# A decoder layer in split fp32: the order of the twelve matmuls in a product

## The chip, the cores and the metric

The kernel runs on one core of a Trainium2 chip. A core has a matrix engine (TensorE, PE in the profile, with its weight loads in a row of their own, PEld), a vector engine (VectorE, DVE), a scalar engine (ScalarE, ACT), a general engine (GpSimd, POOL) and a queue engine (SyncE, SP) that issues most transfers. The engines run side by side, each through its own instructions in order, and wait for one another on semaphores. The metric is the device time of one execution in microseconds, the median of several runs.

## The reference

One layer of a decoder over 2048 positions of width 1024, in fp32. Modulated input, a wide projection, two mixers side by side (sliding-window attention and a causal pool), gates, an output projection and a layer norm:

```python
u = x * (1.0 + scale[:, None, :]) + shift[:, None, :]
h = u @ w_in[l]
q, k, v, a_gate, p_in, p_gate, m_a, m_p = jnp.split(h, offsets, axis=-1)
a = sliding_window_sink_attention(q, k, v, sinks[l], bias, mask) * jax.nn.silu(a_gate)
a = a @ w_attn_proj[l]
p = jnp.einsum('bsgc,gcd->bsgd', multiscale_causal_pool(p_in), w_pool_mix[l]).reshape(B, S, POOL_WIDTH)
p = (p * pool_scale[l]) * jax.nn.silu(p_gate)
p = p @ w_pool_proj[l]
y = jax.nn.sigmoid(m_a) * a + jax.nn.sigmoid(m_p) * p
y = (y @ w_out[l]) * (1.0 + gate[:, None, :])
x = layer_norm(DEEPNORM_ALPHA * x + y, ln_gain[l], ln_bias[l])
```

Nearly all the time goes to the dense products: `u @ w_in` (seven groups of 1024 columns' worth of output tiles and a small k/v group), the two projections and the output product.

## The kernel before

**Split numbers.** TensorE works on fp32r operands here. An fp32 operand is split in two: a high part, rounded by a copy to fp32r (on ACT), and a low part, the rest (`low`, line 130, a subtraction on DVE or POOL). A product of two split operands takes three matmuls: high by high, high by low, low by high (`mm3`, line 136).

**Seven products instead of eight.** A `Quad` (line 244) holds two 128-row weight tiles over the contraction of 1024, and multiplies them with 1024 positions. Seen as blocks it is two by two by two; it is done in the Strassen-Winograd manner with seven block products, named after the moving side's blocks: B11, T1, T2, B21, T3, B22, T4. For each name there is a `set_...` tile in SBUF with four k-tiles, each with a high and a low part of 512 columns. The weight side is summed by POOL (`sum1`, `mid`, `late`) into tile `W` and then split: `pair_split` (line 303) casts 128x1024 numbers on ACT (line 305) and takes the low part on DVE (line 131 by way of 306), into two `w_set` tiles that serve two products each; `half_split` (line 309) does so for one product. There are four `w_set` buffers, used in turn, so a cast waits until PE has read an old tile for the last time.

**A product.** `product` (line 316) multiplies one block: four k-tiles, three matmuls each, twelve matmuls of 128x128 weights by 128x512, all into one PSUM bank (`mm` or `lg` in the profile). Before the change it goes k-tile by k-tile and calls `mm3` for each, so that the weight's low part is first read by the third matmul.

**Stages.** The positions are done in two halves. For each half a ring of gate projections (`first_phase`, `second_phase`) is followed by attention, into whose PE stream the products of 13 further quads are filled, one k-tile at a time (`filling`, which calls `product` with `k, k + 1`). The last stage, from about 1190 us on, has the two projections of each half and the output product. In rings `front` opens a quad (B11, T1), `back` goes on with T2, B21, T3, B22, T4 for two quads in turn, and `finish_pairs` ends the output product. Lines 367, 389 and 420 are DVE adds that read finished products, and each quad's `consume` reads its results out of PSUM.

**What sets the order.** Work beside the products (loads, set splits, sums, stores) hangs on ticks, one per product. PE's instructions keep the order in which the program writes them: all go through `pe`, an `Ordered` wrapper (line 50) that pins each behind the one before. So do calls through `act`, `dve`, `pool` and `sp`. Calls written as `nc.scalar`, `nc.vector`, `nc.gpsimd` and `nc.sync`, which is what `pair_split`, `half_split`, `front`, `back` and most consumers use, are not pinned: the framework's planner sorts them by its own estimate of when each is ready, in the program's order among the ready ones. Semaphore waits come from what each instruction reads and writes.

**Sets.** For each new phase, `set_steps` (line 493) fetches a set in two halves of two k-tiles, through SP, into the place of the old set's low parts, and splits it there. The fetch waits for PE's last read of the part it overwrites.

Of the kernel before, what the change touches and what calls it, by code (L numbers as in the profile page):

```python
# [19 lines left out]
P = 128  # L20
# [39 lines left out]
def kernel(  # L60
# [72 lines left out]
    def mm(*args, **kw):  # L133
        pe.matmul(*args, **kw)

    def mm3(acc, whi, wlo, uhi, ulo, start, stop, **kw):
        mm(acc, whi, uhi, start=start, stop=False, **kw)
        mm(acc, whi, ulo, start=False, stop=False, **kw)
        mm(acc, wlo, uhi, start=False, stop=stop, **kw)
# [176 lines left out]
    def product(acc, w, name, first=False, i0=0, i1=4):  # L316
        t = sets[name]
        hi, lo = w
        for i in range(i0, i1):
            cols = slice(i * P, (i + 1) * P)  # L320
            mm3(
                acc,
                hi[:, cols],
                lo[:, cols],
                t[:, i, 0, :],
                t[:, i, 1, :],
                first and i == 0,
                i == 3,
                skip_group_check=True,
            )  # L330

    def front(ph, q, tick):
        w = pair_split(ph, q.first())
        q.mid()
        a, b = bank(), bank()
        product(a, w[0], "B11", True)
        tick()
        product(b, w[1], "T1", True)
        tick()
        return a, b, None, None  # L340

    def back(ph, grp, opened, nxt, own, tick):
# [5 lines left out]
        for q, (a, b, c, w, *copy) in zip(grp, opened):  # L348
            p5 = ph.p("p5")
            if w is None:  # L350
                c = bank("lg")
                nc.scalar.copy(c, a)
                nc.scalar.copy(p5, b)
                w = pair_split(ph, q.second())[::-1]
                q.late()
                product(c, w[1], "T2")
            else:
                u2 = copy[0] if copy else ph.p("u2")
                if not copy:
                    nc.scalar.copy(u2, a)  # L360
                if c is None:
                    c = bank("lg")
                    product(c, w[1], "T2", True)
                nc.vector.tensor_tensor(c, c, u2, ALU.add)
                nc.scalar.copy(p5, b)
            tick()
            nc.vector.tensor_tensor(b, c, p5, ALU.add)
            if not copy:
                product(a, w[0], "B21")
            tick()  # L370
            q.consume(ph, 0, 0, a)
            st.append((q, b, c, p5))
# [1092 lines left out]
    with Pools("mix", spare=4, p=2, c=8) as ph:  # L1465
# [10 lines left out]
        for n, (raw, i) in enumerate((raw, i) for raw in (ain_d[1], pin_d[1], wo_d) for i in range(4)):  # L1476
            for offset, f in sums_to(ph, raw, i, load_raw(raw, i)):
                at = int(2 + 8 * n + offset)
                i, gi = every[at // 14]
# [78 lines left out]
```

## Time and profile before

| | |
|---|---|
| median of 3 runs | 1722.41 us (1721.44 to 1725.9) |
| the profiled execution | 1724.84 us, of which its span is 1723.1 |
| PE, matmuls | 8056, busy 1659.3 us (96%) |
| PEld, weight loads | 8056, busy 1389.4 us (81%) |
| DVE | busy 1283.1 us (74%) |
| ACT | busy 965.8 us (56%) |
| POOL | busy 1001.9 us (58%) |
| mean granted TensorE clock | 0.991 |

A row of a group names line, engine, operation, the tiles it writes and reads, shapes and count. In order of time a row gives the start, the length of a merged stretch, and in brackets the engine's idle time before it with what ended it. Most instructions are recorded at line 56, the wrapper's, so tiles tell them apart. Matmuls overlap: each is recorded with a length that is longer than the step from one start to the next.

### The profile page before, as it was taken

How to read it: one execution, taken by the hardware profiler on the slowest of the kernel's cores; microseconds unless marked ns; L12 is line 12 of the kernel's file. 1: busy time of each engine (PE TensorE's matmuls, PEld its weight loads, DVE VectorE, ACT ScalarE, POOL GpSimd, SP SyncE). 2: the span in 40 equal slices, each digit the busy share in tenths (PEclk: the TensorE clock that was granted, in tenths of full speed). 3: DMA queues.
4: the chain of work that ended last, by engine and by line, in shares of the span. 5: the costliest groups of instructions: out<-in, count | busy, mean ns of one | idle time of the engine just before them, and what ended most of it. 6: DMA issues, size and time to landing. Idle time of an engine off the chain costs nothing.

```text
span 1723.1 us, 24716 instructions
## 1 busy us (share of the span) xinstructions
PE 1659.3 (96%) x8056; PEld 1389.4 (81%) x8056; DVE 1283.1 (74%) x2288; ACT 965.8 (56%) x2002; POOL 1001.9 (58%) x750
## 2 busy tenths in 40 slices
PE   6899999999999999999999999999999989999996
PEld 5788888888888788887788888888777767778885
DVE  5966665787778768557578777786779886979877
ACT  4644446677677555334567776765645345434452
POOL 2054437686867837863376868595667575523442
PEclk9999999999999999999999999999999999999999
DMA  9388853333433468875533344234988896777442
GB/s 354 126 283 284 220 180 129 117 96 125 142 116 104 129 223 269 299 248 184 197 125 96 113 128 157 83 115 157 339 271 321 301 342 243 292 257 250 159 142 103
DMA packets 188850, 336.79 MB, mean 195 GB/s; under 512 B 18337, under 2 KB 44081, under 8 KB 188721
## 3 DMA queue, kind: packets, MB, share of 16 engines
q1 hardware_dynamic: 185600, 330.96, 56.5%
q10 hardware_dynamic: 3088, 4.23, 1.1%
q8 instruction: 64, 1.05, 0.3%
q14 instruction: 66, 0.53, 0.1%
q0 software_dynamic: 32, 0.02, 0.0%
HBM read 227.96 MB, written 110.33 MB: 196 GB/s over the span
## 4 chain that ended last, share of the span: by engine, by line
PE 44%; DVE 9%; DMA 6%; POOL 5%; issue 4%; ACT 1%; SPq 0%; POOLq 0%; DVEq 0%; ACTq 0%
PE mm L56 29%; PE lg L56 11%; DVE w_set L131 3%; PE pv L56 2%; PE pt L56 2%; DVE set_T L56 1%; POOL nxt L56 1%; POOL w_set L56 1%; DMA set_T<-ain_T 1%; DMA W<-y_d 1%; DVE set_B L56 1%; DVE wide L612 1%; POOL W L56 1%; POOL fin L56 1%; DMA g<-ma_d 1%
## 5 line engine op out<-in xcount | busy, mean ns | idle before, releaser
L56 PE MATMUL mm<-set_B,w_set 128*128 128x512 f32 x2664 | 658.5, 394 | 11.0 <-DVE w_set L131 10.6
L56 PEld LDWEIGHTS mm<-set_B,w_set 128*128 128x128 f32 x2664 | 498.2, 189 | 118.5 <-DVE w_set L131 15.2
L56 PE MATMUL mm<-set_T,w_set 128*128 128x512 f32 x1824 | 456.9, 396 | 4.4 <-POOL w_set L56 1.2
L56 PE MATMUL lg<-set_T,w_set 128*128 128x512 f32 x1728 | 420.5, 393 | 16.4 <-DVE w_set L131 9.0
L56 PEld LDWEIGHTS mm<-set_T,w_set 128*128 128x128 f32 x1824 | 336.8, 189 | 76.9 <-DVE mm L56 5.5
L56 PEld LDWEIGHTS lg<-set_T,w_set 128*128 128x128 f32 x1728 | 324.8, 189 | 90.8 <-DVE w_set L131 13.7
L131 DVE TENSOR_TENSOR w_set<-W,w_set 128x1024 fp32r<-128x1024 f32 x138 | 199.4, 1446 | 153.6 <-ACT w_set L305 143.1
L305 ACT CAST w_set<-W 128x1024 fp32r<-128x1024 f32 x138 | 144.9, 1050 | 258.6 <-PE mm L56 174.2
L56 POOL TENSOR_TENSOR w_set<-W,w_set 128x512 fp32r<-128x512 f32 x132 | 172.1, 1311 | 101.7 <-ACT w_set L56 94.5
L268 POOL TENSOR_TENSOR W<-W,A 128x512 f32<-128x512 f32 x46 | 71.0, 1543 | 252.4 <-ACT w_set L312 58.7
L56 ACT ACTIVATE L<-L,nm 128x257 f32<-128x257 f32 (+1 forms) x256 | 127.1, 498 | 25.8 <-DVE nm L56 20.0
L56 POOL TENSOR_TENSOR W<-W 128x512 f32<-128x512 f32 x82 | 108.4, 1336 | 51.6 <-DVE sm L56 30.3
L56 POOL TENSOR_TENSOR spare<-spare 128x512 f32<-128x512 f32 x68 | 122.4, 1803 | 23.8 <-DMA spare<-pin_B 10.3
L277 POOL TENSOR_TENSOR W<-W 128x512 f32<-128x512 f32 x46 | 69.2, 1504 | 108.8 <-DVE w_set L131 99.7
L56 DVE CUSTOM_DVE_ANT_0 L<-lg,bt,nsink 128x256 f32<-128x256 f32 (+1 forms) x256 | 111.7, 473 | 19.8 <-DMA bt<-e_rep 9.0
L56 ACT CAST w_set<-W 128x512 fp32r<-128x512 f32 (+1 forms) x164 | 100.1, 626 | 37.4 <-POOL W L56 25.8
L56 DVE COPY o<-pv 64x256 f32<-64x256 f32 x128 | 54.3, 424 | 82.3 <-PE pv L56 81.0
L272 POOL TENSOR_TENSOR W<-W 128x512 f32<-128x512 f32 x44 | 72.2, 1645 | 68.7 <-DVE w_set L131 59.7
L56 ACT CAST pth<-pt 128x512 fp32r<-128x512 f32 (+1 forms) x128 | 72.8, 569 | 63.0 <-PE pt L56 62.6
L56 ACT ACTIVATE L<-L,sm 128x256 f32<-128x256 f32 (+1 forms) x128 | 64.3, 503 | 67.9 <-DVE sm L56 67.7
L273 POOL TENSOR_TENSOR W<-W 128x512 f32<-128x512 f32 x44 | 79.3, 1803 | 30.7 <-DMA W<-in_win_dram 27.9
L56 DVE TENSOR_SCALAR L<-L,sm 128x256 f32<-128x256 f32 (+1 forms) x128 | 89.8, 702 | 0.0
(225 smaller groups left out, 2445.2 us busy)
## 6 DMA issues: line engine op xcount, KB each, us to landing
W<-in_win_dram SPq DMA_DIRECT2D x42, 512.0 KB, 5.6
W<-in_win_dram SPq DMA_DIRECT2D x42, 256.0 KB, 4.1
A<-in_win_dram SPq DMA_DIRECT2D x42, 256.0 KB, 4.8
ag_d<-sig SPq DMA_DIRECT2D x32, 256.0 KB, 5.2
pg_d<-sig SPq DMA_DIRECT2D x32, 256.0 KB, 4.8
pg<-pg_d SPq DMA_DIRECT2D x32, 256.0 KB, 3.2
pin_B<-fin SPq DMA_DIRECT2D x32, 256.0 KB, 2.1
ag<-ag_d SPq DMA_DIRECT2D x32, 256.0 KB, 3.0
```

Of the source, the lines that this page charges most:

```text
L56: return lambda *args, **kw: self.tc.keep_in_program_order(op(*args, **kw))
L131: engine.tensor_tensor(dst, src, as32(hi), ALU.subtract)
L268: e.tensor_tensor(self.w[:, 1, :], self.w[:, 2, :], self.a22, ALU.add)
L272: e.tensor_tensor(x[:, 1, :], x[:, 1, :], x[:, 0, :], ALU.subtract)
L273: e.tensor_tensor(x[:, 2, :], x[:, 0, :], x[:, 2, :], ALU.subtract)
L277: e.tensor_tensor(x[:, 3, :], x[:, 3, :], x[:, 1, :], ALU.subtract)
L305: a.copy(by_two(hi), raw)
L612: nc.vector.tensor_tensor(dst, g, dst, ALU.add)
```

## The change

`product` loops over the three kinds of matmul outside and over the k-tiles inside: first the high weight by the set's high part for all k-tiles, then the high weight by the set's low part, last the low weight by the set's high part. `start` and `stop` stay with the first and the last matmul. `mm3` is left to the small weight fold in the first stage.

```diff
     def product(acc, w, name, first=False, i0=0, i1=4):
         t = sets[name]
         hi, lo = w
-        for i in range(i0, i1):
-            cols = slice(i * P, (i + 1) * P)
-            mm3(
-                acc,
-                hi[:, cols],
-                lo[:, cols],
-                t[:, i, 0, :],
-                t[:, i, 1, :],
-                first and i == 0,
-                i == 3,
-                skip_group_check=True,
-            )
+        for n, (part, u) in enumerate(((hi, 0), (hi, 1), (lo, 0))):
+            for i in range(i0, i1):
+                mm(
+                    acc,
+                    part[:, i * P : (i + 1) * P],
+                    t[:, i, u, :],
+                    start=first and i == 0 and n == 0,
+                    stop=i == 3 and n == 2,
+                    skip_group_check=True,
+                )
```

A program run of the kernel calls `product` 324 times for a whole product of four k-tiles, 6 times for two or three of them (in the head), and 762 times for a single k-tile.

## The prediction

> **What bounds the kernel now.** I read the page first, then who waited for whom on PE, then PE's and DVE's instructions in order of time, then the chain of work that ended last.
>
> ```profile
> span 1723.1 us, 24716 instructions
> ...
> PE 1659.3 (96%) x8056; PEld 1389.4 (81%) x8056; DVE 1283.1 (74%) x2288; ACT 965.8 (56%) x2002; POOL 1001.9 (58%) x750
> ```
>
> PE is busy 96% of the span: TensorE bounds the kernel, and a reordering can only give back what PE spends waiting, 64 us, or take more. There are as many weight loads (PEld) as matmuls (8056 each).
>
> ```profile
> PE mm L56 <- DVE w_set L131: 10.6, 9, 4.9
> PE lg L56 <- DVE w_set L131: 9.0, 8, 2.0
> ```
>
> Columns: total us, times, longest. The largest causes are the two rows of `w_set` from line 131: the low half of a weight, made by DVE. Together 19.6 us in 17 waits, at the top of PE's list. PE in order of time shows where in a product the waits fall:
>
> ```profile
> 1242.95 0.61 PE L56 MATMUL lg<-set_T,w_set 128*128 128x512 f32 x2
> 1244.75 2.58 PE L56 MATMUL lg<-set_T,w_set 128*128 128x512 f32 x10 [1.19 <-DVE w_set L131]
> 1247.18 2.88 PE L56 MATMUL mm<-set_B,w_set 128*128 128x512 f32 x12
> 1249.90 0.61 PE L56 MATMUL lg<-set_T,w_set 128*128 128x512 f32 x2
> 1251.67 2.58 PE L56 MATMUL lg<-set_T,w_set 128*128 128x512 f32 x10 [1.16 <-DVE w_set L131]
> ```
>
> Two matmuls, the wait, then ten. The first two of a product use the weight's high part; the third is the first to read its low part. The high part and both parts of the set were there. DVE in the same place shows why the low part is late:
>
> ```profile
> 1245.22 4.16 DVE L56 TENSOR_TENSOR set_B<-set_B 128x1024 fp32r<-128x1024 f32 x2
> 1249.31 2.31 DVE L131 TENSOR_TENSOR w_set<-W,w_set 128x1024 fp32r<-128x1024 f32 x1
> ```
>
> The low part that PE wants from 1249.9 on stands on DVE's queue behind two set splits (4.16 us) and ends at 1251.62; PE goes on at 1251.67.
>
> **The change part by part.** Nothing is added or removed: the same twelve matmuls go to the same PSUM bank, the first with `start`, the last with `stop`. Only products called whole (and six partial ones in the head) change; those that attention fills in go one k-tile at a time, where old and new order agree.
>
> *Price of a matmul.* A product without waits:
>
> ```profile
> 620.31 2.72 PE lg L56 x12
> ```
>
> 2.72 / 12 = 0.227 us each. A whole product shows as 2.88 in order of time because its last matmul counts with its full length: 11 x 0.227 + 0.389. I take the reordered stream at the same step, so PE's work costs 0. Rows for that length and for the two halves of a weight's split, with shortest, median and longest in ns:
>
> ```profile
> L56 PEld LDWEIGHTS mm<-set_B,w_set x2664: 186/188/333, 28.8 to 1707.3; 128*128 128x128 f32 x191
> L56 PE MATMUL mm<-set_B,w_set x2664: 387/389/794, 28.8 to 1707.5; 128*128 128x512 f32 x191
> L305 ACT CAST w_set<-W x138: 1032/1051/1065, 65.3 to 1696.8; 128x1024 fp32r<-128x1024 f32 x138
> L131 DVE TENSOR_TENSOR w_set<-W,w_set x138: 1207/1225/2317, 68.7 to 1697.9; 128x1024 fp32r<-128x1024 f32 x138
> ```
>
> *The wait for the weight's low part moves from the third to the ninth matmul.* Six more matmuls run ahead of it, 6 x 0.227 = 1.36 us. A wait costs more than its bracket: the bracket starts at the previous matmul's end, 0.389 after its start, where the stream would have gone on after 0.227, so 0.16 is added; and the ten matmuls behind a wait take 2.58 where 0.389 + 9 x 0.227 = 2.43 would do, about 0.14 more. The 17 waits cost 19.6 + 17 x 0.30 = 24.7 us. Five exceed the cover:
>
> ```profile
> 69.93 4.03 PE L56 MATMUL lg<-set_T,w_set 128*128 128x512 f32 x10 [1.58 <-DVE w_set L131]
> ...
> 1393.32 4.48 PE L56 MATMUL mm<-set_B,w_set 128*128 128x512 f32 x10 [4.86 <-DVE w_set L131]
> ...
> 1435.19 2.58 PE L56 MATMUL mm<-set_B,w_set 128*128 128x512 f32 x10 [1.53 <-DVE w_set L131]
> ...
> 1469.61 5.38 PE L56 MATMUL lg<-set_T,w_set 128*128 128x512 f32 x22 [1.46 <-DVE w_set L131]
> ...
> 1549.69 6.92 PE L56 MATMUL lg<-set_T,w_set 128*128 128x512 f32 x22 [2.00 <-DVE w_set L131]
> ```
>
> With 0.16 each and 1.36 taken off, 0.38 + 3.66 + 0.33 + 0.26 + 0.80 = 5.4 us stay, with 5 x 0.14 = 0.7. The others vanish. Direct gain: 24.7 - 6.1 = 18.6 us.
>
> *What is late next.* Where DVE itself is the chain, the next low part comes no sooner because PE is ahead, and only the last wait of a row counts.
>
> ```profile
> 1236.47 7.88 DMA set_T<-ain_T
> 1244.36 4.92 DMA g<-ma_d
> 1249.31 2.32 DVE w_set L131
> ...
> 1284.00:1349.00 65.00, 61.86 (x268) 49.69 (x267) 62.55 (x54) 34.72 (x46) 45.06 (x25) 1.00 0.90 323
> ```
>
> The chain reaches the low part of 1249.31 through two transfers, not through PE, so the two waits before it (0.52, shown below, and 1.19, with 0.30 each 2.3 us) give nothing more. The last row is a window: length, then busy PE, PEld, DVE, ACT, POOL, clock, DMA share, GB/s. DVE is busy 62.55 of 65 us there; two waits of it (0.83 and 0.69, with 0.30 each) and a shorter one of 0.3 give nothing, 2.4 us; only the one at its end counts. The waits meant, in order:
>
> ```profile
> 1237.82 2.58 PE L56 MATMUL lg<-set_T,w_set 128*128 128x512 f32 x10 [0.52 <-DVE w_set L131]
> ...
> 1307.22 2.56 PE L56 MATMUL mm<-set_B,w_set 128*128 128x512 f32 x10 [0.83 <-DVE w_set L131]
> ...
> 1335.73 2.57 PE L56 MATMUL lg<-set_T,w_set 128*128 128x512 f32 x10 [0.69 <-DVE w_set L131]
> ...
> 1475.88 2.34 PE L56 MATMUL mm<-set_B,w_set 128*128 128x512 f32 x9 [0.45 <-DVE w_set L131]
> ```
>
> Of the pair at 1469.61 and, 6 us later, 1475.88 (0.45 + 0.30) I count the first, so 0.75 goes. Taken off: 2.3 + 2.4 + 0.8 = 5.5 us. If all these gained after all, the sum would be 5.5 better; rival 2 is the other bound.
>
> *Buffers come free at other times.* The high tile's last read moves from the eleventh to the eighth matmul, 3 x 0.227 = 0.68 us earlier; the low tile's stays the twelfth. ACT's next cast into it can start that much sooner:
>
> ```profile
> ACT w_set L305 <- PE mm L56: 174.2, 72, 9.1
> ...
> DVE w_set L131 <- ACT w_set L305: 143.1, 59, 6.4
> ...
> SPq L56 <- PE mm L56: 23.1, 23, 4.2
> ```
>
> ACT's wait is long because it is early; where a low part was late, the first two matmuls had already run on its high part. I take 0, with 17 x 0.68 = 11.6 better as the end if each late low part came so much sooner. Of a set, the last reads of the low part move from the fifth to the sixth matmul for the first half of the k-tiles (0.23 later) and from the eleventh to the eighth for the second (0.68 earlier). SP waits for these before it fetches the next set into that place (the last row), with all later transfers queued behind it. One such place in the chain:
>
> ```profile
> 1284.18 2.52 PE lg L56 x12
> 1286.69 6.53 DMA set_T<-pin_T
> ```
>
> The chain goes from PE into a set's fetch at 1229.94 and 1523.52 too. Three places: between 3 x 0.23 = 0.7 us lost and 3 x 0.68 = 2.0 gained. I take 1.0 gained, since the second half is issued last. The set's high parts are now read earlier, the second half's from the third matmul instead of the seventh; in the five rows above PE waited for none of them, so 0, at worst 4 x 0.227 = 0.9 us per phase whose first set is just in time.
>
> *The slow clock.* Behind long waits PE runs slowly: ten matmuls took 4.48 us at 1393.32 and 4.03 at 69.93 instead of 2.57, and 22 took 6.92 at 1549.69 instead of 5.3, together 1.9 + 1.5 + 1.6 = 5.0 us. I take 0 and keep 5.0 as the upper end. [...]
>
> *Sum.* -18.6 + 5.5 - 1.0 = -14.1 us. The profiled execution took 1724.84 us (its span 1723.1 and 1.7 around it), which becomes 1710.7. The median of the runs is 2.4 below the profiled one: 1722.41 - 14.1 = 1708.3 us.
>
> **The rivals.**
>
> 1. *The slow stretches go as well.* Then 5.0 more, about 1703 us. For it: all three lie behind waits that get shorter. Against: the longest stays over 3 us.
>
> 2. *DVE takes it back.* In the last third DVE and DMA set the pace:
>
> ```profile
> 1190.00:1560.00 370.00, 351.67 (x1515) 284.81 (x1514) 298.38 (x272) 176.89 (x229) 207.93 (x122) 0.99 0.83 293
> ...
> 88.97 2.56 PE L56 MATMUL mm<-set_B,w_set 128*128 128x512 f32 x10 [0.93 <-DVE w_set L131]
> ...
> 686.41 2.56 PE L56 MATMUL mm<-set_B,w_set 128*128 128x512 f32 x10 [0.37 <-DVE w_set L131]
> ...
> 798.64 2.56 PE L56 MATMUL lg<-set_T,w_set 128*128 128x512 f32 x10 [0.41 <-DVE w_set L131]
> ...
> 802.65 2.56 PE L56 MATMUL mm<-set_B,w_set 128*128 128x512 f32 x10 [1.00 <-DVE w_set L131]
> ```
>
> DVE is busy 298 of 370 us, DMA 83%. If every gain there reappeared as the next wait, only the five earlier waits would be worth anything: 1.36 at 69.93 and, brackets with 0.30 each, 1.23, 0.67, 0.71 and 1.30 at the four rows above; 5.3 us, so 1717. Against: between these waits PE runs for 10 to 40 us without one, and DVE's work there follows on products that end sooner.
>
> 3. *The planner sorts DVE's queue worse (slower).* Only PE's order is fixed by the program in these products; ACT, DVE and POOL are sorted by the planner's own estimate of what is ready. With high tiles free earlier, a low part can be put before the add that reads a finished product, and then the next product waits at its first matmul, where nothing covers it. One such wait now:
>
> ```profile
> 1385.00 3.00 PE L56 MATMUL lg<-set_T,w_set 128*128 128x512 f32 x12 [1.05 <-DVE p L389]
> ```
>
> It costs 1.05 + 0.16 = 1.2 us, like the low part's 1.225. To undo 14.1 us takes 12 of these, to be measurably slower 16; with 20 the time is 1708 + 24 = 1732. For it: 138 low parts of this size, and DVE's order is free. Against: an earlier cast moves low parts forward, which is what PE lacks.
>
> 4. *The weight is no longer reused.* The old order used each high weight twice in a row. [...] If a repeated weight were free to load now, the new order would pay for four loads more per product, at most 0.188 x 4 x 324 whole products = 244 us. Against: 8056 loads for 8056 matmuls, and 2.72 us for twelve with old and new weights mixed leaves no load on the path.
>
> **How the numbers follow.** Forecast (1708, between 1704 and 1716): 0.54. Rival 1: 0.10. Rival 2: 0.18, of which 0.08 just over 0.3% faster and 0.10 within it. Rival 3: 0.16, of which 0.02 within. Rival 4: 0.02. 0.3% (5.2 us) is about what a measurement of this kernel can tell from no change. Faster: 0.54 + 0.10 + 0.08 = 0.72; same 0.12; slower 0.16. The range reaches from 1700, under rival 1, to 1724, over rival 2; most of rival 3 stays out. The likeliest case alone spans 1704 to 1716.
>
> **What would show it.** The two rows of PE's waits for `w_set` L131 shrink from 19.6 to about 6 us in some five waits; PE in order of time breaks such products into eight and four instead of two and ten; twelve matmuls still take 2.72 us; 8056 loads stay. Rival 2 shows as DVE waits at the ninth matmul as long as now; rival 3 as new waits of PE for lines 367, 389 and 420; rival 4 as twelve matmuls above 2.72. I am wrong if PE's other waits grow by what these lose.

## The result and the profile after

The changed kernel takes 1704.49 us (median of 5 runs, 1701.08 to 1705.47), the kernel before 1722.41. The ratio is 0.9886, with a 95% interval from 0.9874 to 0.9897: 1.1% faster. The profiled execution took 1704.85 us, 20.0 less than the one before the change. Its page and the waits of PE:

```profile
span 1703.0 us, 24709 instructions
...
PE 1653.7 (97%) x8056; PEld 1388.5 (82%) x8056; DVE 1280.8 (75%) x2288; ACT 966.7 (57%) x2002; POOL 1007.5 (59%) x750
```

```profile
PE lg L56 <- DVE p L387: 3.8, 3, 2.9
...
PE lg L56 <- DVE w_set L131: 2.2, 3, 0.9
PE mm L56 <- DVE w_set L131: 1.9, 3, 1.1
...
PE lg L56 <- DVE set_T L56: 1.2, 1, 1.2
...
PE mm L56 <- ACT w_set L305: 0.6, 1, 0.6
```

The span is 20.1 us shorter. PE's busy time fell by 5.6 us with the same number of matmuls: fewer of them run behind a wait (6 for the low part instead of 17) or at the slow clock (busy for 21.0 us at a granted clock of 0.50 before, 15.7 after); its time without work fell by the other 14.5. The waits for the low part (line 131) went from 19.6 us in 17 to 4.1 in 6, and some 3 us came back elsewhere: the wait for the reader of T3 (line 389 before, 387 after, since two lines fell away above it) rose from 1.1 to 3.8 us. PE in order of time, at the product that stood at 1387.84 before, and at a wait that is new:

```profile
1380.75 1.97 PE L56 MATMUL mm<-set_B,w_set 128*128 128x512 f32 x8
1383.78 1.21 PE L56 MATMUL mm<-set_B,w_set 128*128 128x512 f32 x4 [1.06 <-DVE w_set L131]
...
1248.45 1.97 PE L56 MATMUL lg<-set_T,w_set 128*128 128x512 f32 x8
1251.18 1.19 PE L56 MATMUL lg<-set_T,w_set 128*128 128x512 f32 x4 [0.75 <-DVE w_set L131]
```

Where a product still breaks for the low part, it breaks into eight and four. The product that stood at 1249.90 before, with a wait of 1.16, now starts at 1243.01 and runs through; the wait of 0.75 is two products later, where none was before. The wait of 1.06 was 4.86 us. A cover of 1.36 us explains only part of that, so DVE must have come to that low part sooner. It did, because the planner put it elsewhere. DVE before the change and after it, at this place (start, length):

```profile
1387.56 2.30 DVE L56 TENSOR_TENSOR set_T<-set_T 128x1024 fp32r<-128x1024 f32 x1
1389.79 1.75 DVE L612 TENSOR_TENSOR wide<-g,wide 128x512 f32<-128x512 f32 x1
1391.45 0.68 DVE L610 TENSOR_TENSOR g<-lg,g 128x512 f32<-128x512 f32 x1
1392.06 1.21 DVE L131 TENSOR_TENSOR w_set<-W,w_set 128x1024 fp32r<-128x1024 f32 x1
```

```profile
1379.68 2.31 DVE L56 TENSOR_TENSOR set_T<-set_T 128x1024 fp32r<-128x1024 f32 x1
1381.91 0.68 DVE L608 TENSOR_TENSOR g<-mm,g 128x512 f32<-128x512 f32 x1
1382.52 1.21 DVE L131 TENSOR_TENSOR w_set<-W,w_set 128x1024 fp32r<-128x1024 f32 x1
1383.65 0.68 DVE L610 TENSOR_TENSOR wide<-g,wide 128x512 f32<-128x512 f32 x1
```

The sum into `wide` and a gate product now follow the low part. In the whole program 61 DVE, 39 ACT, 6 POOL and 11 SP instructions stand in another place than before (the fewest that have to be moved to turn one order into the other); PE's products stand in the same order. So two things changed at once: PE's order inside a product, and the order of the other engines. The experiments take them apart.

### The profile page after: what moved, and what is told of

It is laid out like the page before. It is cut to its first block, busy times and chain, and to the rows that moved or that the text cites. A ratio compares the mean times of both kernels' runs of the same rounds, so it can differ in the third digit from the quotient of the medians.

```text
span 1703.0 us, 24709 instructions
## 1 busy us (share of the span) xinstructions
PE 1653.7 (97%) x8056; PEld 1388.5 (82%) x8056; DVE 1280.8 (75%) x2288; ACT 966.7 (57%) x2002; POOL 1007.5 (59%) x750
## 4 chain that ended last, share of the span: by engine, by line
PE 46%; DVE 9%; issue 5%; DMA 4%; POOL 4%; ACT 1%; SPq 0%; POOLq 0%; DVEq 0%; ACTq 0%
PE mm L56 30%; PE lg L56 12%; DVE w_set L131 2%; PE pv L56 2%; PE pt L56 2%; DVE set_T L56 1%; DVE set_B L56 1%; DVE wide L610 1%; DMA set_T<-pin_T 1%; POOL spare L56 1%; DVE g L608 1%; POOL w_set L56 1%; POOL W L268 1%; DMA g<-ma_d 1%; DVE o L56 0%
## 5 line engine op out<-in xcount | busy, mean ns | idle before, releaser
L56 PE MATMUL lg<-set_T,w_set 128*128 128x512 f32 x1728 | 418.1, 392 | 10.1 <-DVE p L387 3.8
L56 POOL TENSOR_TENSOR W<-W 128x512 f32<-128x512 f32 x82 | 108.3, 1335 | 51.2 <-DVE sm L56 30.3
L277 POOL TENSOR_TENSOR W<-W 128x512 f32<-128x512 f32 x46 | 74.7, 1625 | 95.9 <-DVE w_set L131 86.0
L272 POOL TENSOR_TENSOR W<-W 128x512 f32<-128x512 f32 x44 | 73.9, 1681 | 60.6 <-DVE w_set L131 46.3
L56 DVE TENSOR_TENSOR ptl<-pt,pth 128x512 fp32r<-128x512 f32 (+1 forms) x128 | 85.7, 669 | 2.9 <-ACT pth L56 2.4
```

Of the source, the lines that this page charges most:

```text
L56: return lambda *args, **kw: self.tc.keep_in_program_order(op(*args, **kw))
L272: e.tensor_tensor(x[:, 1, :], x[:, 1, :], x[:, 0, :], ALU.subtract)
L277: e.tensor_tensor(x[:, 3, :], x[:, 3, :], x[:, 1, :], ALU.subtract)
```

## The experiments

A theory of three causes was tested: **cover** (the low part is read six matmuls later), **release** (the high tile is free at the eighth matmul instead of the eleventh, so ACT casts sooner), and **planner** (the new order on DVE and ACT). To hold an order, each kernel below marked "held" chains every instruction of ACT, DVE, POOL and SP behind the one that precedes it in a given order, without adding a semaphore. `ORDER` has one text per engine, with the instruction numbers of that order as differences (cut):

```python
for text in ORDER.values():
    n, prev = 0, None
    for step in text.split():
        n += int(step)
        ins = by.get(f"I-{n}")
        ...
        if prev is not None:
            tc.add_manual_dep(
                ins,
                prev.name,
                mybir.DependencyInfo(mybir.DependencyClass.NoSync, mybir.DependencyReason.DATA),
                reason="pin",
            )
        prev = ins
```

**The new product, the old order held.** The product of the change; all engines but PE as in the kernel before.

> The changed product; ACT, DVE, POOL and SP held in exactly the order they have in the kernel before, so that only PE's order differs from it. Cover theory (the weight's low part is read six matmuls later, which hides DVE's lateness): most of the 17.9 us measured for the change remains, 1704 to 1711 us, and PE's waits for w_set L131 fall from 19.6 us to under 7. Planner theory (the gain comes from the new sorting of DVE's queue): under 5 us of it remains, 1718 to 1724.

Measured: 1713.8 us beside 1724.97, ratio 0.9935 (0.9918 to 0.9951), that is 11 us faster.

```profile
PE mm L56 <- DVE w_set L131: 5.7, 6, 3.2
PE lg L56 <- DVE p L387: 5.0, 5, 2.5
PE lg L56 <- DVE w_set L131: 4.4, 5, 1.6
```

PE's own new order gives a bit over half of the gain. The waits for low parts halve, to 10.1 us in 11, more than the 7 that were expected; the longest is now 3.2 us instead of 4.9, and PE waits 5.0 us for the reader of T3 (1.1 before). The order inside a product gains by itself, as the cover theory has it, but not the whole gain. This run does not part cover from release, since the product has both.

**The old product, the new order held.**

> The product of the kernel before (k-tile by k-tile); ACT, DVE, POOL and SP held in the order that they have in the changed kernel. Cover theory: 1719 to 1727 us, PE's waits for w_set L131 stay between 15 and 25 us. Planner theory: 1705 to 1712.

Measured: 1711.39 us beside 1724.97, ratio 0.9924 (0.9908 to 0.9940): 13 us faster, with TensorE's instructions as they were.

```profile
PE mm L56 <- DVE w_set L131: 6.3, 6, 2.1
PE lg L56 <- DVE w_set L131: 4.8, 7, 1.9
```

```profile
1384.12 0.61 PE L56 MATMUL mm<-set_B,w_set 128*128 128x512 f32 x2
1386.83 2.57 PE L56 MATMUL mm<-set_B,w_set 128*128 128x512 f32 x10 [2.09 <-DVE w_set L131]
```

The planner's order alone takes the waits for low parts from 19.6 to 11.1 us, and the long one from 4.86 to 2.09, with no cover (two matmuls, then ten). Cover theory alone expected no gain here and fails. The two gains, 11 and 13 us, do not add up to the 18 to 20 of the change: both shorten the same waits. The longest, 4.86 us in the kernel before, is 3.2 with the new product alone, 2.1 with the new order alone and 1.1 with both.

**Late release, cover of five, old order held.** The last high by low goes to the very end of a product (shown against the `product` of the change, cut).

```diff
-        for n, (part, u) in enumerate(((hi, 0), (hi, 1), (lo, 0))):
+        todo = [(hi, i, 0) for i in ks] + [(hi, i, 1) for i in ks] + [(lo, i, 0) for i in ks]
+        if len(ks) == 4:
+            todo.append(todo.pop(7))
```

> Order of before on ACT, DVE, POOL and SP. In a product: high by high 4, high by low 3, low by high 4, and the last high by low at the very end. The low part is first read by the eighth matmul (cover of five, 1.13 us), and the high tile's last read is the twelfth matmul, later even than in the kernel before. Cover theory: some 2 us less than the same order with a cover of six, 1706 to 1713. Release theory (the gain comes from the high tile that is free at the eighth matmul, so that ACT casts sooner): the gain is gone, 1719 to 1726.

Measured: 1718.95 us beside 1724.97, ratio 0.9963 (0.9948 to 0.9979), 6 us faster.

```profile
PE mm L56 <- DVE w_set L131: 9.4, 7, 4.2
...
PE lg L56 <- DVE w_set L131: 3.2, 5, 1.2
```

Well above what the cover theory expected, and just under the range of the release theory. With a cover that is one matmul shorter (0.23 us) and a high tile free at the twelfth matmul, 5 of the 11 us are lost. The profile does not show where. Its waits for low parts are 12.6 us in 12, 2.5 more than in the first run above, and one matmul of cover on 12 waits is already 2.7 us; besides, the profiled execution was the fastest of its six (1713.69 us, below the 1715.71 of the first run's profile). That the rest of the 5 us is the release is argued and not shown. This product also reads the low part of the set's last k-tile last, so that part comes free later as well.

**Early release, no cover, old order held.** The first k-tile's three matmuls come first, then the rest by kind. `todo` starts as the list above (cut).

```diff
+        if len(ks) == 4:
+            todo = [todo[n] for n in (0, 4, 8, 1, 2, 3, 5, 6, 7, 9, 10, 11)]
```

> Order of before on ACT, DVE, POOL and SP. In a product the first k-tile's three matmuls come first, as before the change, then three of high by high, three of high by low, three of low by high. The low part is read by the third matmul (no cover); the high tile is free at the ninth instead of the eleventh (0.45 us sooner). Cover theory: 1719 to 1725, waits for w_set L131 as before. Release theory: two thirds of the gain, 1708 to 1713.

Measured: 1721.27 us beside 1724.97, ratio 0.9978 (0.9962 to 0.9995).

```profile
PE mm L56 <- DVE w_set L131: 12.6, 10, 4.9
PE lg L56 <- DVE w_set L131: 8.4, 9, 1.8
```

The waits stay as they were (21.0 us in 19); some 4 us are gained, with an interval from 1 to 6.5. In an order that is held, and without cover, an earlier release is worth little.

**The same product, the planner free.**

> The product with the low part read by the third matmul (no cover) and the high tile free at the ninth, now with the planner free to sort ACT, DVE, POOL and SP (55 DVE and 34 ACT instructions change place against before; 9 and 10 against the changed kernel). With the order of before it gave a ratio of 0.998. If it is the early release of the high tile that makes the planner sort better: near the run with the old product in the new order (0.992), 1708 to 1714 us. If the new order is good only together with the cover, or by the few places in which it differs: 1717 to 1724.

Measured: 1712.06 us beside 1722.29, ratio 0.9938 (0.9923 to 0.9952), 11 us faster.

```profile
PE mm L56 <- DVE w_set L131: 8.1, 6, 3.5
PE lg L56 <- DVE w_set L131: 3.9, 5, 1.7
```

The very same stream on PE gains 4 us when the others keep their places and 11 when the planner may sort them. With an early release and no cover it changes nearly the same places as in the change: 55 DVE and 34 ACT instructions. So without cover this product gains mostly by way of the planner. That the planner sorts so because it reckons ACT's cast, and then the low part, to be ready sooner is what its rule suggests. Its estimates were not looked at, the set's low parts come free at other times too, and the product with the late release was not run with the planner free.

**One low part moved.** The kernel before, every order held, but for one DVE instruction: the low part of 1392.06 goes ahead of the four instructions before it.

> The kernel before, its product untouched, every engine held in its order there, with a single DVE instruction moved: the low part of the weight that PE waits 4.86 us for at 1393.32 goes four places forward, before a gate sum, a set split (2.30 us), a second gate sum and a gate product. If the place of a low part on DVE's queue is what the planner changed to good effect: that wait goes to under 0.5 us and the slow stretch behind it with it, 4 to 7 us faster, 1716 to 1720 beside 1723. If DVE's total work is what holds PE there, so that the order does not matter: the wait reappears within the next products, within 2 us of before.

Measured: 1721.42 us beside 1724.74, ratio 0.9982 (0.9971 to 0.9993), 3 us faster.

```profile
1387.81 2.88 PE L56 MATMUL mm<-set_B,w_set 128*128 128x512 f32 x12
1390.53 2.88 PE L56 MATMUL mm<-set_T,w_set 128*128 128x512 f32 x12
1393.29 0.73 PE L56 MATMUL mm<-set_B,w_set 128*128 128x512 f32 x2
1396.68 2.56 PE L56 MATMUL mm<-set_B,w_set 128*128 128x512 f32 x10 [2.66 <-DVE w_set L131]
1399.08 2.88 PE L56 MATMUL mm<-set_T,w_set 128*128 128x512 f32 x12
1401.80 0.61 PE L56 MATMUL lg<-set_T,w_set 128*128 128x512 f32 x2
1402.88 2.56 PE L56 MATMUL lg<-set_T,w_set 128*128 128x512 f32 x10 [0.47 <-DVE w_set L131]
```

The wait of 4.86 us and its slow stretch are gone, and two products later there is one of 2.66, then one of 0.47: 4.86 became 3.1. The product after the long wait started at 1397.64 before and starts at 1390.53, 7.1 us sooner; behind the two new waits 3.3 us are left (1408.56 before, 1405.28 here), which is about what the runs gained (1 to 5 us). Part of the wait was the place on the queue and part was DVE's whole backlog there, so both expectations were half right.

The total of PE's waits for low parts did not fall in this execution: 19.7 us in 17, as before. Up to the moved instruction the two kernels are the same, and yet these waits come to 9.1 us in the kernel before and to 10.2 here. A difference of about one microsecond between two totals is therefore no more than the scatter between executions.

**The weight repeated.** Order of the changed kernel held; in a product, high by high and high by low of a k-tile in turn, then low by high.

```diff
+        todo = [(hi, i, u) for i in ks for u in range(2)] + [(lo, i, 0) for i in ks]
```

> ACT, DVE, POOL and SP in the order of the changed kernel. In a product high by high and high by low of the same k-tile follow one another (the high weight twice in a row, as in the kernel before), low by high last, as in the change: same cover, same release, only the repetition of the weight differs. If a repeated weight costs PE nothing less: as the changed kernel within 3 us, 1702 to 1709, twelve matmuls still 2.72 us. If a reload has a price: faster than the changed kernel by more than 5 us.

Measured: 1702.2 us beside 1724.74, ratio 0.9871 (0.9856 to 0.9886). Since that was a little under the changed kernel, both ran again side by side.

> The changed kernel once more, as the mark for the three runs beside it: 1702 to 1707 us, ratio to before 0.987 to 0.990.

> As before: the changed kernel's order on ACT, DVE, POOL and SP, high by high and high by low of a k-tile in turn, low by high last. If it was faster than the changed kernel for a reason: 2 us or more below it again. If that was noise: within 2 us of it.

Measured: the changed kernel 1705.96 us, 0.9894 (0.9876 to 0.9911); the repeated weight 1705.65 us, 0.9902 (0.9887 to 0.9917), both beside 1722.29. No difference. Twelve matmuls of it, in the chain:

```profile
618.96 2.72 PE lg L56 x12
621.68 2.72 PE mm L56 x12
```

There are 8056 loads here too: a weight used twice in a row cost PE the same here as two weights, 2.72 us for twelve matmuls.

**More cover in front.** In `front`, the sixteen matmuls of B11 and T1 on the high weight, then the eight on the low one. `product` gets a parameter for the kinds that it does; the planner is free.

```diff
-        product(a, w[0], "B11", True)
+        product(a, w[0], "B11", True, kinds=(0, 1))
+        product(b, w[1], "T1", True, kinds=(0, 1))
+        product(a, w[0], "B11", True, kinds=(2,))
         tick()
-        product(b, w[1], "T1", True)
+        product(b, w[1], "T1", True, kinds=(2,))
         tick()
```

> The changed kernel, and in front, where B11 and T1 share one weight split, both products' eight matmuls on the high part come first, then low by high of B11, then of T1: sixteen matmuls run ahead of the low part instead of eight (3.6 us of cover). Four of the changed kernel's six waits for w_set L131 stand at B11 (0.85, 1.22, 0.34 and 0.15 us). Cover theory: these vanish, 2 to 4 us faster than the changed kernel, 1699 to 1704. If the waits only move to the next product: 1703 to 1708.

Measured: 1705.92 us beside 1724.74, ratio 0.9889 (0.9874 to 0.9905): as the changed kernel.

```profile
PE lg L56 <- DVE p L389: 2.9, 4, 1.8
PE mm L56 <- ACT w_set L305: 2.2, 2, 2.0
PE lg L56 <- DVE w_set L131: 1.5, 3, 0.7
```

The waits at B11 are gone: no row of `mm` for the low part is left, where the changed kernel has three (0.69, 1.06 and 0.17 us, not four as expected). In their place PE waits 2.2 us for the high part itself (0.6 in the changed kernel). The planner moved some 50 instructions of ACT as well, so PE's order is not the only difference here.

**Low parts first.** The changed kernel with planner priority for the low parts of `pair_split`.

```diff
-        low(d, by_two(lo), raw, by_two(hi))
+        with tc.high_priority(offset=200):
+            low(d, by_two(lo), raw, by_two(hi))
```

> The changed kernel, with the low parts made in pair_split given priority in the planner, so that DVE takes one as soon as it is ready (22 DVE instructions change place). If the place of low parts is what counts: 1 to 6 us faster than the changed kernel, 1698 to 1703. If the cover already hides what is left: within 2 us of it; slower, if set splits and product readers are now late (waits for lines 365 and 387).

Measured: 1705.13 us beside 1724.74, ratio 0.9887 (0.9871 to 0.9902): no difference. PE's waits for low parts stay at 3.9 us in 5.

**Both variants together.** The joint front with each weight repeated, in the order that the planner gave the joint front.

> The two variants together: in front sixteen matmuls on high weights (high by high and high by low of a k-tile in turn) ahead of the eight on low ones, other products as in the run above, ACT, DVE, POOL and SP in the order that the planner gave the joint front. If both help: 1698 to 1702 us, 3 or more below the changed kernel. If the last waits just move on to the readers of products (lines 365 and 387 of the changed kernel): 1702 to 1707.

Measured: 1705.08 us beside 1722.29, ratio 0.9898 (0.9885 to 0.9912). Nothing that was tried beats the changed kernel clearly.

## Why the prediction came out as it did

The time, 1704.5, lies in the range and 4 us under the forecast of 1708.3. The direction and the main mechanism were right; the sum came close by luck, because one missing term and one overrated term partly cancel.

*Price of a matmul: right.* Twelve take 2.72 us before the change, after it and with each weight repeated, and there are still 8056 loads. Rival 4 is refuted by the runs with a repeated weight. Every matmul has a load of its own in all three (8056 loads for 8056 matmuls).

*The wait moves to the ninth matmul: right in kind.* The products break into eight and four. The direct gain was put at 18.6 us; the waits fell by 15.5 us, and eleven fewer of them at 0.30 make 18.8. But this agreement is luck, since the product's order did only part of it: with the old order held, waits fell by 9.5 and, with six fewer at 0.30, that makes 11.3.

*What is late next: one wait was missing.* After taking off 5.5 us for places where DVE is the chain, the new product in the old order was to give 14.1; that experiment measured 11, with an interval (8.5 to 14.1) that just reaches it. What was missing is the wait at the first matmul of T4: it stands behind the reader of T3, has no cover, and rose from 1.1 us (2.2 with one of 1.18 that the profile puts down to ACT) to 5.0 when PE got there sooner. With the planner free, some of what was taken off came after all: between the products that started at 1233.08 and at 1249.90 before, PE gained 3.2 us, where the sum counted two waits (2.3 us) as worth nothing.

*Buffers come free at other times: the step that failed.* I took 0 for the earlier release of the high tile, looking only at ACT in its given order. Held in that order an earlier release gains about 4 us; left to the planner it gains 11 without any cover. The change gives 18 to 20 us by the ratios and the held one 11, so 7 to 8 us come by way of the planner on top of the new product. Taken the other way round, the new order alone gives 13 and the new product adds 5 to 6.5. How much of this is the high tile's release, and how much the set's parts that also come free at other times, stays open.

*Rival 3 had the mechanism and the wrong sign.* The planner did sort DVE's queue anew, as that rival says, but its new order as a whole, with the old product, is 13 us faster. The prediction named this side under "against" and gave it no term. The longer waits at T4 are not the new order's doing either: with the old order held they are 5.0 us in 5, in the changed kernel 3.8 in 3. The longest of the changed kernel, and DVE ahead of it in the changed kernel and then in the kernel before:

```profile
1337.13 5.46 PE L56 MATMUL lg<-set_T,w_set 128*128 128x512 f32 x12 [2.85 <-DVE p L387]
```

```profile
1331.24 1.77 DVE L131 TENSOR_TENSOR w_set<-A,w_set 128x512 fp32r<-128x512 f32 x1
1332.93 0.68 DVE L608 TENSOR_TENSOR g<-mm,g 128x512 f32<-128x512 f32 x1
1333.54 1.18 DVE L131 TENSOR_TENSOR w_set<-A,w_set 128x512 fp32r<-128x512 f32 x1
1334.64 1.75 DVE L610 TENSOR_TENSOR wide<-g,wide 128x512 f32<-128x512 f32 x1
1336.31 0.68 DVE L387 TENSOR_TENSOR p<-lg,p 128x512 f32<-128x512 f32 x1
```

```profile
1338.99 0.68 DVE L610 TENSOR_TENSOR g<-mm,g 128x512 f32<-128x512 f32 x1
1339.60 1.17 DVE L131 TENSOR_TENSOR w_set<-A,w_set 128x512 fp32r<-128x512 f32 x1
1340.69 1.78 DVE L612 TENSOR_TENSOR wide<-g,wide 128x512 f32<-128x512 f32 x1
1342.40 1.77 DVE L131 TENSOR_TENSOR w_set<-A,w_set 128x512 fp32r<-128x512 f32 x1
1344.10 0.68 DVE L389 TENSOR_TENSOR p<-lg,p 128x512 f32<-128x512 f32 x1
```

In both orders two low parts, a gate product and a sum into `wide` stand before the add that T4 waits for. T4 waited 1.18 us here already before the change, and 2.53 with the new product in the old order. PE reaches the product before this T4 9.7 us sooner than before the change (1331.13 instead of 1340.86), the add comes only 7.8 sooner.

*Rival 2 (DVE takes it back) did not hold.* The stage where it should have:

```profile
1190.00:1560.00 370.00, 363.64 (x1583) 297.54 (x1582) 311.16 (x283) 189.20 (x242) 217.63 (x123) 0.99 0.84 302
```

In the same stretch of 370 us PE now does 1583 matmuls where it did 1515, and DVE is busy 311 instead of 298: DVE had room. The 68 more, at 0.227 us each, are 15 of the 20 us between the two profiles, so most of the gain comes from the stage that this rival gave nothing.

*The slow clock: a term of the sum that I set to 0.* The three stretches of the prediction went (5.0 us), and a new one came behind the wait of 2.85 above, twelve matmuls in 5.46 us instead of 2.88. Two more, which the prediction did not see, cancel: one at 585.13 before and one at 1158.62 after, both 3.41 us at a granted clock of 0.50, behind waits in attention (1.07 and 1.09 us before, 0.67 and 1.09 after). Some 2 us were gained on balance.

*Not tested by itself:* the 1.0 us for set fetches that start sooner.

## What to carry to other kernels

In a split product, do everything that needs the part made first, and read the late part last. Here that cost PE nothing (twelve matmuls took 2.72 us in both orders), and six matmuls moved ahead (1.36 us) took 1.4 us off one wait (1.58 became 0.20) and 1.6 off the longest (4.86 became 3.22), with the old order held. When instructions on other engines are sorted by a planner, a change of one engine's order is also a change of theirs: hold the order to see what the change itself is worth, and count an earlier release as a possible gain, not as zero. When a cover has taken most of a wait, look at who waits at the first instruction of a group, since nothing of the group runs ahead of that (here the first matmul of T4, which waited 2.85 us at 1337.13 in the changed kernel, 1.18 at the same place before).

## What the runs showed of the hardware that was not expected

The length of a wait alone did not tell whether PE ran slowly behind it. In the kernel before, a wait of 2.00 us was followed by a slow stretch (22 matmuls in 6.92 us); in the experiment with one low part moved, a wait of 2.66 was not (ten in 2.56); in the changed kernel one of 2.85 was (twelve in 5.46). Two neighbouring stretches at the wait of 2.00, then two at the wait of 2.66 (start and end; length, then busy PE, PEld, DVE, ACT, POOL, clock, DMA share, GB/s):

```profile
1547.70:1551.10 3.40, 1.41 (x6) 1.19 (x7) 3.40 (x4) 0.43 (x1) 1.63 (x2) 1.00 1.09 378
1551.12:1554.50 3.38, 3.38 (x9) 2.60 (x9) 3.35 (x6) 1.04 (x1) 1.35 (x1) 0.50 1.04 405
...
1392.00:1395.40 3.40, 2.03 (x9) 1.13 (x7) 3.37 (x5) 3.06 (x4) 3.40 (x3) 1.00 0.87 276
1395.50:1398.80 3.30, 2.12 (x9) 1.78 (x10) 3.30 (x3) 1.80 (x3) 3.30 (x3) 1.00 0.99 365
```

In the first row PE was busy 1.41 of 3.40 us at a granted clock of 1.00; in the next the granted clock was 0.50. Around the wait of 2.66 PE was busy 2.03 of 3.40 us and 2.12 of 3.30, and the granted clock was 1.00 in both rows. At the wait of 2.85 it was 0.50 for 6.83 us, from 1336.11 in the changed kernel on. What decides between these cases is not shown by these three waits.
